# Seven products instead of eight in nine more pairs of a feed-forward, and down-projection sums that begin at 2x in PSUM

## The chip, the core and the metric

The kernel runs on one core of a Trainium2 chip. The metric is device time in microseconds (us) from the start of the program to its end. Times quoted are the median of three runs, or one profiled execution where a trace is read.

The engines go by the profile's names: PE multiplies matrices (PEld is its weight load), DVE and ACT are the vector and the scalar engine, POOL a third elementwise engine, SP issues most transfers.

## The reference

A decoder layer over 256 tokens of width 2048, in float32: a feed-forward, a mixer (sliding-window attention beside RWKV-7), cross-attention, a second feed-forward, a last RMS norm. Both feed-forwards have an inner width of 5632 and compute

```python
def swiglu(h, w_gate, w_up, w_down):
    return (jax.nn.silu(h @ w_gate) * (h @ w_up)) @ w_down

x = x + 0.5 * swiglu(rms_norm(x, ffn1_norm[l]), ffn1_w_gate[l], ffn1_w_up[l], ffn1_w_down[l])
...
x = x + 0.5 * swiglu(rms_norm(x, ffn2_norm[l]), ffn2_w_gate[l], ffn2_w_up[l], ffn2_w_down[l])
```

## The kernel before

**A product.** Every float32 operand is split into a high part (ACT casts it to fp32r, L365, or L373 for the sums below) and a low part (DVE subtracts, L366 or L374). One product of a 128x128 block of activations with a 128x512 block of weights is then three matmuls: high times high (L442), low weight times high (L443), high weight times low activation (L444), added up in one PSUM bank of 128x512 (`times`).

**Pairs of seven.** The 256 tokens are two tiles, t = 0 and 1. `product_pair` works on two weight blocks of 512 columns at once: w_gate and w_up for the same columns (`gate_and_up`), or two column blocks of w_down (`down`). It goes through K in pairs q of two 128-row chunks. A plain pair takes 2 tiles x 2 weight blocks x 2 chunks = 8 products, 24 matmuls. A pair in the set `seven` takes 7 products, 21 matmuls (Strassen's scheme in Winograd's form), named p1 to p7. For that DVE builds four sums of the two weight blocks (L394 to L397, 128x512 each) and these are split again (`two_parts`: two casts on ACT, two subtractions on DVE of 128x1024); in return half of the split of the second weight block falls away (`split_unit(u, slice(1, 2))`). Sums of activations are made once per activation (`combinations`): four per seven pair, and two for each plain pair that comes ahead of the last seven pair.

**Banks.** PSUM has three rings: `mm` (p1, p3, p5; three banks), `acc` (p2, p4, q; three), `tr` (p6, p7, and the transposes of `feat`; two). p5's early plain products go to a bank of their own, `q`, where the activations' sums were not made for these pairs.

**Blocks.** Inner width 5632 is 11 blocks of 512, j = 0 to 10, in three groups of 4, 4 and 3. Block 0 is done plain; blocks 1 to 10 each are one `gate_and_up` of 8 pairs. After a group come two `down` calls (columns 0 to 1023, then 1024 to 2047) over the group's inner columns: 8 pairs, or 6 in the third group. In the second feed-forward the very last call is replaced by plain products. Before, gate and up take seven products in pairs 0, 2, 4 (first feed-forward) or 0, 2, 3, 4 (second, where pair 3's weight sums were computed in the mixer and are loaded); `down` takes them in 2, 4, 6 (groups of 4, first call) and in 2, 4 elsewhere.

**Order.** `next_item` splits the weights of one pair ahead of the pair that PE is on. Other work (transposes of a finished block, sums of activations, norms) is in generators that `bg.tick()` advances between products; `middle`, after the last seven pair of a block, spawns the transposes of the block before (`c["next"]`, L582 and L583). The order of each engine's queue is set when the program is built: instructions are moved there by their estimated readiness, within what the dependencies allow. On the chip each engine runs its queue in order.

**The end of `down`.** With u2 and u3 as helper tiles, ACT copies p1 (L606), and DVE adds p1, p5, p6, p7 and q up and then adds half of each sum to x: twelve DVE instructions of 128x512 a call (L603, L611 to L613).

## Time and profile before

| | us |
|---|---|
| median of 3 runs (2217.76 to 2218.34) | 2218.07 |
| the profiled execution, whole | 2216.97 |
| its span, first to last instruction | 2215.2 |
| PE busy | 2200.2 |
| weight loads busy | 1817.0 |
| DVE busy | 1829.0 |
| ACT busy | 1250.0 |

The first feed-forward takes the span from 5 to 710 us, the mixer and cross-attention 710 to 1508, the second feed-forward 1509 to 2206. "Busy" is a share of the span over stages of different kinds; a matmul's record lasts longer than the time to the next one's start, since they are pipelined, so a rate is read from starts. DVE and ACT records overlap a little in the same way. In a line of the timeline the bracket at the end gives the idle time ahead of an instruction and what ended it.

### The profile page before, as it was taken

Reading aid. Unit: us, or ns where it says so; the run is one execution under the profiler, and the core shown is the slowest. Engines: PE = TensorE matmul, PEld = TensorE weight load, DVE = VectorE, ACT = ScalarE, POOL = GpSimd, SP = SyncE. Lnnn points to the kernel's source line nnn. Section 1 sums busy time; section 2 is a strip of 40 time slices with the busy share of each in tenths; the row PEclk is TensorE's granted clock in tenths of the full one; section 3 lists DMA queues with packets and bytes.
Section 4 is the critical chain, followed back from the end, with each engine's and each line's share of the span. In section 5 each row is a group of like instructions: output and inputs, shape, how many; then the busy total and the mean of one; then the engine's idle time right before and its main releaser. Section 6 shows DMA issues by size and latency. Waiting matters only on the chain.

```text
span 2215.2 us, 28140 instructions
## 1 busy us (share of the span) xinstructions
PE 2200.2 (99%) x10520; PEld 1817.0 (82%) x10520; DVE 1829.0 (83%) x2348; ACT 1250.0 (56%) x1621; POOL 107.0 (5%) x185
## 2 busy tenths in 40 slices
PE   9999999999999999999999999999999999999998
PEld 7888888888888877788888888888888888888886
DVE  7999988898989476977667666558999999999997
ACT  7555555555556477644544546556565565555654
POOL 0000000000000000000331130001000000000000
PEclk9999999999999999999999999999999999999999
DMA  8555555555556545676768687547665666665573
GB/s 306 199 207 198 194 200 201 198 199 194 200 194 204 178 130 165 197 237 210 223 224 287 209 273 270 183 164 280 220 221 190 212 227 211 214 208 208 200 244 135
DMA packets 231560, 466.02 MB, mean 210 GB/s; under 512 B 15520, under 2 KB 17920, under 8 KB 231424
## 3 DMA queue, kind: packets, MB, share of 16 engines
q1 hardware_dynamic: 222256, 438.08, 58.4%
q0 software_dynamic: 7648, 23.52, 3.5%
q10 hardware_dynamic: 1520, 2.63, 0.3%
q8 instruction: 82, 1.34, 0.3%
q14 instruction: 54, 0.44, 0.1%
HBM read 440.49 MB, written 23.59 MB: 209 GB/s over the span
## 4 chain that ended last, share of the span: by engine, by line
PE 94%; DVE 3%; DMA 1%; issue 1%; ACT 1%; SPq 0%; POOLq 0%; POOL 0%; DVEq 0%; ACTq 0%
PE acc L442 19%; PE acc L443 19%; PE acc L444 19%; PE mm L443 8%; PE mm L444 8%; PE mm L442 8%; PE tr L443 2%; PE tr L630 2%; PE tr L442 2%; PE tr L444 2%; PE mm L1425 1%; DVE lo L366 1%; DMA raw<-in_ffn_w_up_dram 1%; PE tr L1355 0%; ACT hi L365 0%
## 5 line engine op out<-in xcount | busy, mean ns | idle before, releaser
L365 ACT CAST hi<-raw 128x1024 fp32r<-128x1024 f32 (+1 forms) x768 | 755.1, 993 | 687.7 <-PE acc L444 485.9
L366 DVE TENSOR_TENSOR lo<-raw,hi 128x1024 fp32r<-128x1024 f32 (+1 forms) x768 | 878.8, 1147 | 291.8 <-ACT hi L365 289.3
L442 PE MATMUL acc<-hi,xhi 128*128 128x512 f32 (+1 forms) x1134 | 445.7, 394 | 2.0 <-DVE ga L1278 1.5
L443 PE MATMUL acc<-lo,xhi 128*128 128x512 f32 (+1 forms) x1134 | 439.9, 388 | 0.8 <-DVE lo L366 0.8
L444 PE MATMUL acc<-hi,xlo 128*128 128x512 f32 (+1 forms) x1134 | 439.7, 388 | 0.0
L442 PEld LDWEIGHTS acc<-hi,xhi 128*128 128x128 f32 x1134 | 213.2, 188 | 47.8 <-issue 3.1
L444 PEld LDWEIGHTS acc<-hi,xlo 128*128 128x128 f32 x1134 | 212.9, 188 | 43.5 <-issue 0.4
L443 PEld LDWEIGHTS acc<-lo,xhi 128*128 128x128 f32 x1134 | 213.4, 188 | 42.7 <-DVE lo L366 2.2
L373 ACT CAST thi<-raw 128x1024 fp32r<-128x1024 f32 x192 | 200.3, 1052 | 69.1 <-DVE raw L396 45.0
L374 DVE TENSOR_TENSOR tlo<-raw,thi 128x1024 fp32r<-128x1024 f32 x192 | 232.1, 1217 | 0.9 <-ACT thi L373 0.3
L442 PE MATMUL mm<-hi,xhi 128*128 128x512 f32 x402 | 156.6, 389 | 0.1
L443 PE MATMUL mm<-lo,xhi 128*128 128x512 f32 x402 | 156.5, 389 | 0.0
L444 PE MATMUL mm<-hi,xlo 128*128 128x512 f32 x402 | 156.4, 389 | 0.0
L444 PE MATMUL acc<-hi,hlo 128*128 128x512 f32 x372 | 145.4, 391 | 0.0
L443 PE MATMUL acc<-lo,hhi 128*128 128x512 f32 x372 | 145.3, 391 | 0.0
L442 PE MATMUL acc<-hi,hhi 128*128 128x512 f32 x372 | 145.0, 390 | 0.0
L442 PEld LDWEIGHTS mm<-hi,xhi 128*128 128x128 f32 x402 | 75.4, 188 | 16.2 <-ACT hi L365 0.5
L443 PEld LDWEIGHTS mm<-lo,xhi 128*128 128x128 f32 x402 | 75.5, 188 | 15.8
L444 PEld LDWEIGHTS mm<-hi,xlo 128*128 128x128 f32 x402 | 75.5, 188 | 15.7
L442 PEld LDWEIGHTS acc<-hi,hhi 128*128 128x128 f32 x372 | 69.9, 188 | 14.3
L443 PEld LDWEIGHTS acc<-lo,hhi 128*128 128x128 f32 x372 | 69.8, 188 | 14.3
L444 PEld LDWEIGHTS acc<-hi,hlo 128*128 128x128 f32 x372 | 69.9, 188 | 14.0
(443 smaller groups left out, 3526.6 us busy)
## 6 DMA issues: line engine op xcount, KB each, us to landing
raw<-in_ffn_w_down_dram SPq DMA_DIRECT2D x88, 1024.0 KB, 5.2
raw<-in_ffn_w_gate_dram SPq DMA_DIRECT2D x84, 1024.0 KB, 5.1
raw<-in_ffn_w_up_dram SPq DMA_DIRECT2D x78, 1024.0 KB, 6.0
raw<-in_w_in_dram SPq DMA_DIRECT2D x136, 512.0 KB, 3.8
raw<-in_w_out_dram SPq DMA_DIRECT2D x32, 512.0 KB, 4.7
raw<-sums SPq DMA_DIRECT2D x20, 512.0 KB, 6.2
raw<-in_w_proj_attn_dram SPq DMA_DIRECT2D x16, 512.0 KB, 4.0
raw<-in_w_proj_rwkv_dram SPq DMA_DIRECT2D x16, 512.0 KB, 5.7
```

What stands on the lines that cost most here:

```text
L365: at["hi"] = act.copy(hi[:, s], raw[:, s])
L366: at["lo"] = dve.tensor_tensor(lo[:, s], raw[:, s], f32(hi[:, s]), ALU.subtract)
L373: act.copy(hi[:], v[:])
L374: dve.tensor_tensor(lo[:], v[:], f32(hi[:]), ALU.subtract)
L442: pe.matmul(o, xh, hi, start=first, stop=False, **how)
L443: pe.matmul(o, xh, lo, start=False, stop=False, **how)
L444: pe.matmul(o, xl, hi, start=False, stop=last, **how)
L630: pe.transpose(b[:, o : o + P], tok[:, t, col : col + P], ident[:])
L1425: pe.matmul(vb[to, (o + k) * P : (o + k + 1) * P][:, r], lhs(k, e), v[:, k, r], start=v is u and k + e == 0, stop=True, **ek,)
```

## The change

Five blocks of gate and up in the first feed-forward (3, 5, 7, 9, 10) take seven products in pair 6 as well. For them the activations' sums of pair 6 are made too, those of pair 5 are not, so pair 5's share of p5 goes to bank q and DVE adds q in at the end. In groups of four the second `down` call takes seven products in pair 6 as well, in both feed-forwards.

`down` no longer adds x at the end for each bank: before its first product, ACT writes 2x into the banks of p2, p4, p3 and q, the products add onto that, and the end takes half of each bank. u2 and u3 are not used there any more; eight DVE instructions a call remain, and ACT has four more. A seven pair now waits for its own sums of activations only, not for all of them. Two 128x128 tiles that nothing reads go.

```diff
@@ -37,6 +37,7 @@
 
 
 SEVEN, SEVEN_DOWN = (0, 2, 4), ((2, 4, 6), (2, 4))
+SEVEN_MORE, MORE = (0, 2, 4, 6), (3, 5, 7, 9, 10)
 SEVEN_2, STAGED = (0, 2, 3, 4), (3,)
 
 STAGE_AT = [266 + 2 * n for n in range(10)]
@@ -89,13 +90,14 @@
                 for w in (wg, wu):
                     yield w, 0, KD, 0, 512
             else:
-                yield (wg, wu), 0, KD, (j * 512, j * 512), SEVEN_2 if last else SEVEN
+                seven = SEVEN_2 if last else SEVEN_MORE if j in MORE else SEVEN
+                yield (wg, wu), 0, KD, (j * 512, j * 512), seven
         yield (wd, wd), 4 * j0, 4 * nj, (0, 512), SEVEN_DOWN[nj < 4]
         if last and (j0, nj) == GROUPS[-1]:
             for n in (2, 3):
                 yield wd, 4 * j0, 4 * nj, n * 512, 512
         else:
-            yield (wd, wd), 4 * j0, 4 * nj, (1024, 1536), SEVEN_DOWN[1]
+            yield (wd, wd), 4 * j0, 4 * nj, (1024, 1536), SEVEN_DOWN[nj < 4]
 
 
 def weight_plan(a):
@@ -194,7 +196,6 @@
-    cpool.tile([P, P], F32, name="shift")
@@ -239,7 +240,6 @@
-    cpool.tile([P, P], F32, name="pad")
@@ -451,21 +451,19 @@
                 k + i == 0, k + i == nk - 1,
             )
 
-    def combinations(sp, x: Act, seven, name, ready=lambda: True, early=True, n=0):
-
-
-
-        pairs = [q for q in range(max(seven) + 1) if early or q in seven]
-        n = n or sum(4 if q in seven else 2 for q in pairs)
+    def combinations(sp, x: Act, seven, name, ready=lambda q: True, less=(), n=0):
+
+
+
+        pairs = sorted((*seven, *less))
+        n = n or 4 * len(seven) + 2 * len(less)
         parts = [sp.tile([P, n, P], F32R, tag=name + e, name=name + e) for e in ("hi", "lo")]
-        c = {"parts": parts, "at": {}, "done": False, "seven": seven, "early": early}
+        c = {"parts": parts, "at": {}, "seven": seven, "less": less}
 
         def work():
             o = 0
-            while not ready():
-                yield
             for q in pairs:
-                while not {2 * q, 2 * q + 1} <= x.done:
+                while not ({2 * q, 2 * q + 1} <= x.done and ready(q)):
                     yield
                 t = wp.tile([P, KU, 512], F32, tag="raw", name="raw", bufs=4)
                 v = t[:, 0].rearrange("p (k t n) -> p k t n", k=2, t=2)
@@ -494,12 +492,10 @@
                 c["at"][q] = o
                 o += n
                 yield
-            c["done"] = True
-
         bg.spawn("mem", work())
         return c
 
-    def product_pair(x: Act, c, w, first, middle, out):
+    def product_pair(x: Act, c, w, first, middle, out, onto=()):
 
 
 
@@ -512,6 +508,11 @@
         b, begun = {}, set()
         rings = {"p1": mm, "p3": mm, "p5": mm, "p2": acc, "p4": acc, "q": acc}
 
+        for to, there in onto:
+            b[to] = rings[to]()
+            act.activation(b[to][:], there, AF.Copy, scale=2.0)
+            begun.add(to)
+
         def add(to, x_, w_, last=False):
             if to not in b:
                 b[to] = rings.get(to, tr)()
@@ -531,7 +532,7 @@
         for q in range(nk // KU):
             k = KU * q
             if q in seven:
-                bg.until(lambda: c["done"] and (q > min(seven) or not bg.groups["feat"][1]))
+                bg.until(lambda: q in c["at"] and (q > min(seven) or not bg.groups["feat"][1]))
                 g, u, s = next_item()
                 end = q == max(seven)
                 ta, tb = s
@@ -552,8 +553,8 @@
             g, u = next_item()
             early, last = q < max(seven), q == nk // KU - 1
             for to, t, wt in (("p2", 0, g), ("p4", 1, g), ("p3", 0, u), ("p5", 1, u)):
-                less = to == "p3" and early and c["early"]
-                if to == "p5" and early and not c["early"]:
+                less = to == "p3" and early and q in c["less"]
+                if to == "p5" and early and q not in c["less"]:
                     to = "q"
                 for i in range(KU):
                     add(
@@ -589,36 +590,36 @@
                 act.activation(hb[:, t], hb[:, t], AF.Silu, scale=r[t])
             else:
                 v = u3 if t else u2
-                dve.tensor_tensor(v[:], b[to][:], v[:], ALU.add)
+                for z in (to, "q") if t and "q" in b else (to,):
+                    dve.tensor_tensor(v[:], b[z][:], v[:], ALU.add)
                 dve.scalar_tensor_tensor(hb[:, t], v[:], r[t], hb[:, t], ALU.mult, ALU.mult)
 
         product_pair(x, c, w, first, middle, out)
         return hb
 
-    def down(sp, h: Act, c, w, xs):
-
-        u2, u3 = sums_of(sp)
-
-        def half(x_, v):
-            dve.scalar_tensor_tensor(x_, v, 0.5, x_, ALU.mult, ALU.add)
+    def down(h: Act, c, w, xs):
+
+        (x00, x01), (x10, x11) = xs
+
+        def half(x_, v, y):
+            dve.scalar_tensor_tensor(x_, v, 0.5, y, ALU.mult, ALU.add)
 
         def first(b):
-            act.copy(u3[:], b["p1"][:])
-            half(xs[0][0], b["p1"][:])
-            half(xs[1][1], b["q"][:])
+            act.activation(x00, b["p1"][:], AF.Copy, scale=0.5)
 
         def middle(b):
-            dve.tensor_tensor(u2[:], b["p6"][:], u3[:], ALU.add)
-            dve.tensor_tensor(u3[:], b["p7"][:], u2[:], ALU.add)
-            dve.tensor_tensor(u2[:], b["p5"][:], u2[:], ALU.add)
-            half(xs[1][0], u3[:])
-            half(xs[1][1], u3[:])
-            half(xs[0][1], u2[:])
+            half(x01, b["p6"][:], x00)
+            half(x10, b["p7"][:], x01)
+            half(x01, b["p5"][:], x01)
+            half(x11, b["q"][:], x10)
 
         def out(b, to):
-            half(xs[int(to in ("p4", "p5"))][int(to in ("p3", "p5"))], b[to][:])
-
-        product_pair(h, c, w, first, middle, out)
+            x_ = xs[int(to in ("p4", "p5"))][int(to in ("p3", "p5"))]
+            half(x_, b[to][:], x_)
+
+        product_pair(
+            h, c, w, first, middle, out, (("p2", x00), ("p4", x10), ("p3", x01), ("q", x11))
+        )
 
     def feat(tok, cols):
 
@@ -727,8 +728,12 @@
                 sp.tile(shape, dt, tag=tag, name=tag, bufs=bufs)
         begun = at["item"]
         c = combinations(
-            sp, norm.x, SEVEN_2 if last else SEVEN, "c",
-            lambda: at["item"] > begun + (4 if last else 7) and not (last and norm.r is None),
+            sp, norm.x, SEVEN_2 if last else SEVEN_MORE, "c",
+            lambda q: (
+                at["item"] > begun + (4 if last else 26 if q > 4 else 7)
+                and not (last and norm.r is None)
+            ),
+            less=(1,) if last else (1, 3),
         )
         c["next"] = []
         for gi, (j0, nj) in enumerate(GROUPS):
@@ -736,7 +741,7 @@
                 [sp.tile([P, 16, T], F32R, tag="hhi", name="hhi")],
                 [sp.tile([P, 16, T], F32R, tag="hlo", name="hlo")], 16,
             )
-            ch = combinations(sp, h, SEVEN_DOWN[nj < 4], "d", early=False, n=12)
+            ch = combinations(sp, h, SEVEN_DOWN[nj < 4], "d", n=12)
 
             def transposed(hb, c):
                 banks = [feat(hb, [2 * q * P, (2 * q + 1) * P]) for q in range(2)]
@@ -787,7 +792,7 @@
                             )
                             done(m, t, cs)
                     continue
-                down(sp, h, ch, wd, [[col(t, n + i) for i in range(2)] for t in range(2)])
+                down(h, ch, wd, [[col(t, n + i) for i in range(2)] for t in range(2)])
                 if end:
                     done(n)
                     done(n + 1)
```

The change moves instructions on DVE and PE; two places are shown, as the engines' queues hold them.

DVE, first feed-forward, before: the end of block 5, from the last sum after its third seven pair. lo is the low part of a weight tile, hlo that of transposed results (tr is the bank they come from), tlo that of a weight sum; L394 to L397 make the weight sums of the next block's first pair.

```order
L581 TENSOR_TENSOR u<-mm,u 128x512
L366 TENSOR_TENSOR lo<-raw_2689,hi 128x1024
L636 TENSOR_TENSOR hlo<-tr,hhi 128x512 x2
L366 TENSOR_TENSOR lo<-raw_2737,hi 128x1024
L394 TENSOR_TENSOR raw<-raw_2820,raw_2772 128x512
L395 TENSOR_TENSOR raw<-raw_2820 128x512
L396 TENSOR_TENSOR raw<-raw_2820,raw 128x512
L366 TENSOR_TENSOR lo<-raw_2689,hi 128x1024
L397 TENSOR_TENSOR raw<-raw_2772,raw 128x512
L374 TENSOR_TENSOR tlo<-raw,thi 128x1024
L366 TENSOR_TENSOR lo<-raw_2737,hi 128x1024
L374 TENSOR_TENSOR tlo<-raw,thi 128x1024
```

After, DVE at the same place, now with a fourth seven pair (pair 6) just behind it; u and hb hold the block's sums and its result.

```order
L582 TENSOR_TENSOR u<-mm,u 128x512
L374 TENSOR_TENSOR tlo<-raw,thi 128x1024
L366 TENSOR_TENSOR lo<-raw_2794,hi 128x1024
L366 TENSOR_TENSOR lo<-raw_2843,hi 128x512
L374 TENSOR_TENSOR tlo<-raw,thi 128x1024
L589 TENSOR_TENSOR hb<-acc,hb 128x512
L637 TENSOR_TENSOR hlo<-tr,hhi 128x512
L589 TENSOR_TENSOR hb<-acc,u 128x512
L637 TENSOR_TENSOR hlo<-tr,hhi 128x512
L594 TENSOR_TENSOR u<-mm,u 128x512 x2
L595 SCALAR_TENSOR_TENSOR hb<-u,rs,hb 128x512
L594 TENSOR_TENSOR u<-acc,u 128x512
```

Before, the two hlo of the block before are read out of tr two pairs ahead of the block's end, in front of the next block's weight sums; after, they stand behind these (both tlo), within the last pair, and a third L594 adds q.

PE, before: the first seven pair of the first `down` call of group 0 (dhi and dlo are the two parts of its sums of activations, hhi and hlo those of the activations themselves).

```order
L442 MATMUL tr<-thi,dhi 128x512 x2
L442 MATMUL mm<-hi,hhi 128x512
L443 MATMUL mm<-lo,hhi 128x512
L444 MATMUL mm<-hi,hlo 128x512
L443 MATMUL tr<-tlo,dhi 128x512
L444 MATMUL tr<-thi,dlo 128x512
L443 MATMUL tr<-tlo,dhi 128x512
L444 MATMUL tr<-thi,dlo 128x512
```

After, PE at the same pair (its p1, p2 and p3 are already under way when the first row is reached):

```order
L442 MATMUL mm<-hi,dhi 128x512
L442 MATMUL acc<-hi,hhi 128x512 x2
L443 MATMUL mm<-lo,dhi 128x512
L444 MATMUL mm<-hi,dlo 128x512
L442 MATMUL mm<-hi,hhi 128x512
L442 MATMUL tr<-thi,dhi 128x512 x2
L442 MATMUL mm<-hi,hhi 128x512
L443 MATMUL tr<-tlo,dhi 128x512
L444 MATMUL tr<-thi,dlo 128x512
L443 MATMUL tr<-tlo,dhi 128x512
L444 MATMUL tr<-thi,dlo 128x512
```

Before, the first matmul with a low weight sum (tlo) is the 54th of the `down` call, five behind the first with a high one (thi); after it is the 64th, since products of this pair that need no weight sum, and the next pair's high parts, are taken ahead.

## The prediction

> **What bounds the kernel now.** The page's first rows, its shares of the span, and the chain that ended last come first.
>
> ```profile
> span 2215.2 us, 28140 instructions
> PE 2200.2 (99%) x10520; PEld 1817.0 (82%) x10520; DVE 1829.0 (83%) x2348; ACT 1250.0 (56%) x1621; POOL 107.0 (5%) x185
> PE 94%; DVE 3%; DMA 1%; issue 1%; ACT 1%; SPq 0%; POOLq 0%; POOL 0%; DVEq 0%; ACTq 0%
> ```
>
> PE is busy 99% of the time and makes up 94% of the chain. Busy alone doesn't say whether a matmul fewer is worth its time, so the rate has to be seen. PE's timeline at the head of group 0's first `down` call shows a stretch without a gap, and then the first seven pair:
>
> ```profile
> 184.63 0.39 PE L444 MATMUL mm<-hi,hlo 128*128 128x512 f32 x1
> ...
> 191.43 0.39 PE L444 MATMUL acc<-hi,hlo 128*128 128x512 f32 x1
> ...
> 192.57 0.39 PE L444 MATMUL mm<-hi,hlo 128*128 128x512 f32 x1
> 192.93 0.50 PE L443 MATMUL tr<-tlo,dhi 128*128 128x512 f32 x1
> 193.27 0.39 PE L444 MATMUL tr<-thi,dlo 128*128 128x512 f32 x1
> ```
>
> Between the first two rows lie 30 steps in 6.80 us: 0.2267 us from one matmul's start to the next. At 192.57 the next start comes after 0.36 us, and the one behind it after 0.34: together 0.25 us more than two plain steps. That is what a low part (tlo) that is late by a moment costs: the only loss in some 40 us.
>
> The same question by stage is asked of the table by windows (PE, PEld, DVE, ACT busy): blocks 5 and 6, group 1's gate and up as a whole, its two `down` calls, and a block of the second feed-forward.
>
> ```profile
> 306.90:349.00 42.10, 42.10 (x191) 34.96 (x190) 38.42 (x47) 23.98 (x28) 0.00 (x0) 1.00 0.58 200
> 349.00:391.20 42.20, 42.20 (x192) 35.02 (x191) 38.01 (x49) 23.17 (x27) 0.00 (x0) 1.00 0.57 199
> 264.70:433.40 168.70, 168.70 (x758) 139.80 (x757) 149.78 (x183) 94.91 (x106) 0.00 (x0) 1.00 0.58 200
> 433.40:475.70 42.30, 42.30 (x191) 34.67 (x190) 40.76 (x54) 23.25 (x26) 0.00 (x0) 1.00 0.58 198
> 475.70:518.20 42.50, 42.50 (x189) 35.21 (x188) 40.14 (x49) 21.87 (x23) 0.00 (x0) 1.00 0.58 199
> 1847.00:1889.00 42.00, 42.00 (x189) 34.33 (x189) 41.07 (x53) 25.48 (x30) 0.00 (x0) 1.00 0.63 219
> ```
>
> A block of gate and up takes 42.2 us (168.7 / 4), in which DVE works 37.4 (149.78 / 4), so 89%; in `down` it works 40.1 to 40.8 of 42.4, 95% and more. ACT has some 18 us free everywhere. So PE sets the pace, at the full clock (the 1.00), and DVE is the one behind it with little room.
>
> **What is removed.** A seven pair has 21 matmuls where a plain one has 24. Five blocks get one more seven pair, and so do four `down` calls (groups 0 and 1 of both feed-forwards): 9 x 3 = 27 matmuls fewer. At 0.2267 us that is 6.1 us, all on the path, as no gap stands around them. The transposes and loads stay as they were (the same weights come in; SP's queue only issues them).
>
> The Trainium skill has another price for the step ("TensorE: Matmul & The Clock Gate", Back-to-back issue gap: about 216 ns for 512 columns, warm). By it the saving would be 5.8 us; the trace's 226.7 ns decides here, and the sum goes by that.
>
> **What is added on DVE and ACT.** DVE's own timeline just ahead of that seven pair carries the prices:
>
> ```profile
> 175.75 1.22 DVE L366 TENSOR_TENSOR lo<-raw,hi 128x1024 fp32r<-128x1024 f32 x1 [1.49 <-ACT hi L365]
> 178.43 1.23 DVE L366 TENSOR_TENSOR lo<-raw,hi 128x1024 fp32r<-128x1024 f32 x1 [0.26 <-ACT hi L365]
> 179.57 1.28 DVE L592 TENSOR_TENSOR u<-mm,u 128x512 f32<-128x512 f32 x2
> ...
> 187.71 0.28 DVE L481 TENSOR_TENSOR raw<-raw 128x128 f32<-128x128 f32 x1
> 187.91 0.68 DVE L395 TENSOR_TENSOR raw<-raw 128x512 f32<-128x512 f32 x1
> ...
> 190.46 0.68 DVE L493 TENSOR_TENSOR dlo<-raw,dhi 128x512 fp32r<-128x512 f32 x1
> 191.06 0.68 DVE L397 TENSOR_TENSOR raw<-raw,raw 128x512 f32<-128x512 f32 x1
> 191.66 1.22 DVE L374 TENSOR_TENSOR tlo<-raw,thi 128x1024 fp32r<-128x1024 f32 x1
> 192.79 0.68 DVE L366 TENSOR_TENSOR lo<-raw,hi 128x512 fp32r<-128x512 f32 x1
> 193.40 1.22 DVE L374 TENSOR_TENSOR tlo<-raw,thi 128x1024 fp32r<-128x1024 f32 x1
> ```
>
> From start to start an instruction of 128x512 takes 0.60 us (190.46, 191.06, 191.66), one of 128x1024 1.13 (191.66, 192.79), one of 128x128 0.20. One more seven pair costs DVE four sums and two low parts, less half a low part: 4 x 0.60 + 2 x 1.13 - 0.53 = 4.1 us. In the five blocks comes the addition of q, 0.6. So such a block asks DVE for 37.4 + 4.7 = 42.1 us, while PE's part of it falls to 42.2 - 0.7 = 41.5. DVE is 0.6 us short in each. Blocks 4, 6 and 8 between them leave it 4.8 us (42.2 - 37.4); only 9 and 10 follow each other. On the total alone, the split of a pair ahead takes 0.6 us up. So the total costs nothing; what costs is the order.
>
> `down` gives DVE four instructions a call back, 2.4 us, and where a call gets a third seven pair it pays 4.1: 40.1 + 1.7 = 41.8 of PE's 41.8 on the busiest reading of the second call, but with no loss seen at 95%. PE waited for none of the instructions taken out, so their going brings nothing by itself.
>
> ACT gets four writes of 2x into PSUM a call. No row shows such a write; the nearest are the copy out of PSUM and the scaled copy in SBUF:
>
> ```profile
> L606 ACT COPY u<-mm 128x512 f32<-128x512 f32 x11 | 6.5, 587 | 10.4 <-PE mm L444 10.4
> L1744 ACT ACTIVATE x<-x,rs x4: 706/714/724, 2205.1 to 2209.7; 128x512 f32<-128x512 f32 x4
> ```
>
> So 4 x 0.59 to 0.71, 2.3 to 2.8 us in a call in which ACT has some 19 free. The write has to wait for its bank, and the casts of the next weights stand behind it. The banks of p2 and p4 come free with the first two half-additions of the call before, 2 x 6 products' matmuls ahead of its end; the new p2 is needed 18 matmuls, 4.1 us, after its old bank was full, and DVE's addition and ACT's write need 0.6 + 0.7. It costs nothing unless DVE stands some 2.5 us behind there.
>
> **Where the order costs.** Two places, both shown in the queues above.
>
> First, the first `down` of each group of the first feed-forward, behind blocks 3, 7 and 10, each of which now has its fourth seven pair. There the low parts of the block before (two, 1.2 us), the sums of activations made from them (0.6 + 4 x 0.2 + 0.6 = 2.0) and q (0.6) have moved behind the last seven pair: 3.8 us of DVE work more ahead of the first tlo that `down` needs. Against it stand the 1.75 us that DVE idles there now (1.49 + 0.26 in the brackets), and ten matmuls that PE takes ahead, 2.3 us. On balance nothing is lost. If the idle time can't be used, 3.8 - 2.3 = 1.5 us are lost in each. I take 0.5, nearer the low end, since the idle time is in the trace: 3 x 0.5 = 1.5 us.
>
> Second, PE's queue holds many more seven pairs in which products are taken out of their written order around a late low part: 42, where there were 15. Six of the 27 belong to the first place. Each of the others costs between nothing (the reordering hides it all) and the 0.25 us of the row at 192.57. Being ordered around the lateness is what makes most of them free; I take a quarter of the price: 21 x 0.06 = 1.3, and for the two starts of blocks 4 and 8 in the second feed-forward, which is at 98% of DVE already (41.07 of 42.0), 0.1 each, 1.5 in all. The bounds are 0 and 21 x 0.25 = 5.3.
>
> **The sum.** -6.1 + 1.5 + 1.5 = -3.1 us. The profiled execution, 2216.97 us whole with 2215.2 of span and 1.8 around it, would be 2213.9. The median stands 1.1 above that execution, so 2218.07 - 3.1 = 2215.0. With every bound at its best it is 2218.07 - 6.1 = 2212.0, at its worst 2218.07 - 6.1 + 4.5 + 5.3 = 2221.8. About 0.2%, 4.4 us, is what a measurement of this kernel can tell from no change: 2213.6 and 2222.5.
>
> **The rivals.**
>
> *Nothing is lost.* The order hides all that DVE is late, as it does in the 40 us around 192.57 but for 0.25. For it: group 1 shows a DVE at 95% in `down` without loss. Against: the five blocks ask for over 100%. 2212.0.
>
> *Each late low part costs its price.* Then 27 x 0.25 = 6.6 us come back and it is 2218.07 - 6.1 + 6.6 = 2218.6: no change. For it: the one place of the row paid in full although PE's order already went around it. Against: there are 15 such places now, and PE is still without gaps over whole blocks.
>
> *DVE sets the pace: slower.* Its place is the end of the five blocks. The transposed results leave the two tr banks only behind the next block's weight sums, and p6 and p7 of that block, or of `down`, need these banks. If DVE comes there late by what the block has more than before, 4.7 us, and its idle time elsewhere can't be used since it is bound to ACT's casts, and these to PE's releases, then each of the five blocks pays 4.7: 23.5 - 6.1, 2235.5. It decides from the point at which 10.5 of the 23.5 us are paid, 2.1 a block. The rows that tie them:
>
> ```profile
> DVE lo L366 <- ACT hi L365: 289.3, 258, 3.5
> ACT hi L365 <- PE acc L444: 485.9, 356, 3.9
> ```
>
> For it: these are DVE's longest waits, 289 us, and behind them ACT's for PE. Against: in a block DVE comes to its first tlo some us ahead, and 0.6 us short is not 2.1.
>
> The Trainium skill would lean this way ("Perfetto Trace Analysis", Identifying the Most-Contended Engine: TensorE is to be judged by the busy share of its weight loads, the others by occupancy, and the highest is worked on first). By it DVE's 83% stands above PE's 82%, and work put on DVE would show. The starts 0.2267 us apart without gaps speak against it on the whole, the 100% in five blocks for it there.
>
> That the change doesn't do what it says is no case: the queue of PE holds 27 matmuls fewer.
>
> **How the numbers follow.** The forecast, some of the saving given back: 0.46, its own range 2213.0 to 2217.2. Nothing lost: 0.32. Each paid in full: 0.10. DVE's pace: 0.12. The likeliest is 2215.0. The range reaches over the first three, from 2211.8 to 2220.5, and leaves out DVE's pace and little else. Faster by over 0.2%: nearly all of "nothing lost" and the low end of the forecast, 0.31 + 0.06 = 0.37. Slower: 0.12. Within: 0.51.
>
> **What would show it.** In the profile after, the matmuls still 0.227 apart, 27 fewer; block 5 at 41.5 to 42 us with DVE above 41; the first seven pair of each first `down` with a gap of up to some 0.8 us ahead of its L443; L513 with its 44 writes off the chain. The forecast is wrong if PE's gaps in the two feed-forwards grow by less than 1.5 us or more than 5, or if the rest of the program moves at all: nothing between the two feed-forwards changes place.

## The result and the profile after

The changed kernel takes 2225.91 us (median of 7 runs, 2224.03 to 2226.27), the kernel before 2218.22 (7 runs, 2217.76 to 2219.14). The ratio is 1.0032, interval 1.0022 to 1.0042: 7.7 us slower, where 3.1 us faster had been forecast. With the 6.1 us of the matmuls that are gone, 13.8 us were lost, not 3.0.

The page of the profiled execution (2226.11 us) opens with the span, the busy time of each engine and the chain that ended last:

```profile
span 2224.4 us, 28208 instructions
PE 2199.9 (99%) x10493; PEld 1809.7 (81%) x10493; DVE 1841.4 (83%) x2369; ACT 1283.6 (58%) x1684; POOL 107.2 (5%) x185
PE 84%; DVE 8%; DMA 4%; ACT 2%; issue 1%; SPq 0%; POOLq 0%; POOL 0%; DVEq 0%; ACTq 0%
```

PE's records are 27 fewer, as the queue says. Its busy share, 99%, says nothing of the loss; the chain does: PE falls from 94% to 84%, DVE rises from 3% to 8% and DMA from 1% to 4%.

The table by windows (PE, PEld, DVE, ACT busy) for group 1: its gate and up, and its first and second `down` call:

```profile
267.66:436.80 169.14, 168.09 (x750) 138.13 (x749) 159.44 (x194) 97.98 (x112) 0.00 (x0) 1.00 0.60 202
437.03:481.80 44.77, 43.29 (x191) 34.64 (x190) 42.53 (x59) 26.63 (x33) 0.00 (x0) 1.00 0.53 180
481.80:523.58 41.78, 41.78 (x185) 34.36 (x184) 35.84 (x44) 23.33 (x25) 0.00 (x0) 1.00 0.59 194
```

Gate and up takes 169.1 us where it took 168.7 with six matmuls more, DVE works 159.4 of them, 94%, where it was 149.8. The first `down` has grown from 42.3 to 44.8 us.

Where the time goes is read best from PE's own timeline. Here it is at the first `down` of group 0, whose first matmul starts at 181.07 (before, at 179.86):

```profile
194.28 0.39 PE L442 MATMUL mm<-hi,dhi 128*128 128x512 f32 x1
194.51 0.39 PE L442 MATMUL acc<-hi,hhi 128*128 128x512 f32 x1
195.58 0.50 PE L442 MATMUL acc<-hi,hhi 128*128 128x512 f32 x1 [0.68 <-ACT hi L365]
196.47 0.50 PE L443 MATMUL mm<-lo,dhi 128*128 128x512 f32 x1 [0.39 <-DVE lo L366]
...
197.26 0.61 PE L442 MATMUL tr<-thi,dhi 128*128 128x512 f32 x2
198.33 0.50 PE L442 MATMUL mm<-hi,hhi 128*128 128x512 f32 x1 [0.46 <-ACT hi L365]
198.81 0.50 PE L443 MATMUL tr<-tlo,dhi 128*128 128x512 f32 x1
```

Starts that should lie 0.23 us apart lie 1.07 and 0.89 apart, 0.85 ahead of the row at 198.33 (from the second matmul of the row at 197.26) and 0.48 behind it. In PE's queue products that were expected to be ready first stand ahead of their written order; then there are no more of them, and PE waits for hi, lo, hi and tlo in turn. The first `down` of groups 1 and 2 has the same four steps (1.07, 0.86, 0.83 and 0.47 us in both, to 0.02). DVE's timeline shows why (line, operation, in brackets the idle time before it):

```profile
187.61 0.74 DVE L595 SCALAR_TENSOR_TENSOR hb<-u,rs,hb 128x512 f32<-128x512 f32 x1
190.17 1.23 DVE L366 TENSOR_TENSOR lo<-raw,hi 128x1024 fp32r<-128x1024 f32 x1 [1.81 <-ACT hi L365]
191.32 1.28 DVE L637 TENSOR_TENSOR hlo<-tr,hhi 128x512 fp32r<-128x512 f32 x2
192.51 0.68 DVE L472 TENSOR_TENSOR raw<-hhi,hlo 128x512 f32<-128x512 f32 x1
193.11 0.69 DVE L394 TENSOR_TENSOR raw<-raw,raw 128x512 f32<-128x512 f32 x1
...
197.54 1.22 DVE L374 TENSOR_TENSOR tlo<-raw,thi 128x1024 fp32r<-128x1024 f32 x1
```

The last instruction of the block (L595) starts 6.5 us after the `down` call's first matmul. Before, the second of two such stood there:

```profile
180.77 1.41 DVE L593 SCALAR_TENSOR_TENSOR hb<-u,rs,hb 128x512 f32<-128x512 f32 x2
179.86 0.39 PE L442 MATMUL acc<-hi,hhi 128*128 128x512 f32 x1
```

That one started at about 181.4, 1.6 us after 179.86. So DVE comes 5 us later to the block's end. Behind that it idles 1.81 us ahead of 190.17, since the low part at the head of its queue waits for a cast, and ACT's cast for PE to free its buffer:

```profile
189.09 1.05 ACT L365 CAST hi<-raw 128x1024 fp32r<-128x1024 f32 x1 [1.90 <-PE acc L444]
```

Behind it stand the low parts of the block that has just ended and the sums of activations for pair 6 (L637, L472), and only then the weights' sums (L394) that the first tlo needs. That tlo starts 16.5 us after the call's first matmul (197.54 less 181.07); before, it was 11.8 (191.66 less 179.86). It is 4.7 us later, and PE has 2.3 us of other matmuls to put in: 2.4 us are lost.

The second place is the start of a group, 2 to 3 us in. PE, and DVE around it:

```profile
270.18 0.39 PE L444 MATMUL acc<-hi,xlo 128*128 128x512 f32 x1
271.27 0.47 PE L442 MATMUL acc<-thi,xhi 128*128 128x512 f32 x1 [0.70 <-DVE x L605]
```

```profile
259.35 0.69 DVE L394 TENSOR_TENSOR raw<-raw,raw 128x512 f32<-128x512 f32 x1 [2.35 <-DMA raw<-in_ffn_w_up_dram]
...
270.44 1.28 DVE L605 SCALAR_TENSOR_TENSOR x<-acc,x 128x512 f32<-128x512 f32 x2
```

PE waits for an accumulator that the additions of the second `down`'s last pair (L605) release. DVE had idled 2.35 us for the weights of the next block's pair 0; when they landed, eight additions of `down` (L605) and the sums and low parts of pair 0 came due together. At the start of block 6, behind block 5 with its fourth seven pair, it is the same with the additions of the block (0.5 us lost; at block 10 it is 0.3):

```profile
342.00 0.69 DVE L394 TENSOR_TENSOR raw<-raw,raw 128x512 f32<-128x512 f32 x1 [1.77 <-DMA raw<-in_ffn_w_up_dram]
353.23 0.50 PE L442 MATMUL acc<-hi,xhi 128*128 128x512 f32 x1 [0.34 <-DVE hb L589]
```

The profiled execution also came to its first seven pair 1.3 us later than that of before. PE's rows there, of before, after, `seeds` and `seeds_third` (the first two experiments below):

```profile
52.08 0.73 PE L442 MATMUL tr<-thi,chi 128*128 128x512 f32 x2 [0.26 <-ACT thi L373]
53.42 0.73 PE L442 MATMUL tr<-thi,chi 128*128 128x512 f32 x2 [0.26 <-ACT thi L373]
53.21 0.74 PE L442 MATMUL tr<-thi,chi 128*128 128x512 f32 x2 [0.26 <-ACT thi L373]
52.05 0.73 PE L442 MATMUL tr<-thi,chi 128*128 128x512 f32 x2 [0.26 <-ACT thi L373]
```

The last two kernels have the same code up to there and differ by 1.2 us, so this is a matter of the run and no part of the 13.8.

For the whole, each stage's length on PE's timeline less 0.2267 us for each of its matmuls gives an excess: what the stage loses, and the transposes of finished blocks on top, about 0.11 us each from start to start. They make 0.9 us of a `down` of groups 0 and 1 (8 transposes), 2.6 of gate/up 1 (24), 1.7 of gate/up 2 (16) and 3.5 of down 2 (32; before 2.6, as 24), so the kernel before loses next to nothing from the first `down` on in the first feed-forward, and a difference between two rows is what counts. This is the excess in us in one profiled execution of each kernel, for those below too (`down` stands for a group's two calls; the 0.8 us of the eight more transposes in the third group's `down` come back at the head of the mixer):

| kernel | down 0 | gate/up 1 | down 1 | gate/up 2 | down 2 | second ffn, gate/up 1 |
|---|---|---|---|---|---|---|
| before | 1.2 | 2.7 | 1.2 | 1.8 | 3.1 | 3.5 |
| after | 3.6 | 4.8 | 3.8 | 3.7 | 6.2 | 4.6 |
| seeds | 1.2 | 2.7 | 1.2 | 1.8 | 4.4 | 3.5 |
| seeds_third | 1.2 | 3.5 | 1.2 | 2.1 | 4.0 | 4.5 |
| more59 | 1.7 | 4.5 | 1.2 | 3.3 | 4.3 | 5.0 |
| more_two | 3.6 | 3.5 | 3.6 | 2.3 | 6.3 | 3.7 |
| late_sums | 1.4 | 4.2 | 1.4 | 3.7 | 4.4 | 4.9 |
| third_245 | 0.9 | 2.8 | 0.9 | 1.8 | 4.0 | 3.7 |
| after_245 | 2.5 | 3.4 | 2.4 | 2.7 | 6.3 | 4.0 |
| more3710_245 | 2.5 | 2.8 | 2.4 | 1.8 | 6.3 | 4.3 |
| blocks_0245 | 1.3 | 4.1 | 1.5 | 3.5 | 4.3 | 4.6 |
| late_245 | 2.9 | 3.4 | 2.9 | 2.6 | 4.5 | 4.1 |
| all_0245 | 1.4 | 4.0 | 1.4 | 3.2 | 4.7 | 4.7 |
| three_0245 | 1.5 | 2.8 | 1.5 | 1.8 | 4.4 | 4.0 |

From before to after the first `down` calls lose 2.4 and 2.6 us and the third, against `seeds`, 1.8: 6.9 us together, half of all. Gate/up 1 and 2 lose 2.0 and 1.9 more, at the group starts and at blocks 6 and 10, and gate/up 1 of the second feed-forward 1.0: there it isn't the group's start but the start of block 7 and two pairs behind it (steps of 0.72 at 1902 us and 0.41 at 1918 us).

### The profile page after: what moved, and what is told of

The parts are those of the page before. It is cut to its first block, busy times and chain, and to the rows that moved or that the text cites. A ratio compares the mean times of both kernels' runs of the same rounds, so it can differ in the third digit from the quotient of the medians.

```text
span 2224.4 us, 28208 instructions
## 1 busy us (share of the span) xinstructions
PE 2199.9 (99%) x10493; PEld 1809.7 (81%) x10493; DVE 1841.4 (83%) x2369; ACT 1283.6 (58%) x1684; POOL 107.2 (5%) x185
## 4 chain that ended last, share of the span: by engine, by line
PE 84%; DVE 8%; DMA 4%; ACT 2%; issue 1%; SPq 0%; POOLq 0%; POOL 0%; DVEq 0%; ACTq 0%
PE acc L442 17%; PE acc L443 17%; PE acc L444 17%; PE mm L443 7%; PE mm L444 7%; PE mm L442 7%; DVE lo L366 3%; PE tr L443 2%; PE tr L444 2%; PE tr L631 2%; PE tr L442 2%; DMA raw<-in_ffn_w_up_dram 2%; DMA raw<-in_ffn_w_down_dram 2%; PE mm L1430 1%; ACT hi L365 1%
## 5 line engine op out<-in xcount | busy, mean ns | idle before, releaser
L373 ACT CAST thi<-raw 128x1024 fp32r<-128x1024 f32 x210 | 219.1, 1051 | 70.0 <-DVE raw L396 42.4
L374 DVE TENSOR_TENSOR tlo<-raw,thi 128x1024 fp32r<-128x1024 f32 x210 | 254.5, 1218 | 1.4 <-ACT thi L373 0.9
L443 PE MATMUL mm<-lo,xhi 128*128 128x512 f32 x377 | 146.9, 390 | 0.0
L442 PE MATMUL mm<-hi,xhi 128*128 128x512 f32 x377 | 146.8, 390 | 0.0
L444 PE MATMUL mm<-hi,xlo 128*128 128x512 f32 x377 | 146.8, 389 | 0.0
L394 DVE TENSOR_TENSOR raw<-raw,raw 128x512 f32<-128x512 f32 x95 | 65.2, 686 | 29.8 <-DMA raw<-in_ffn_w_up_dram 15.2
L442 PEld LDWEIGHTS mm<-hi,xhi 128*128 128x128 f32 x377 | 70.8, 188 | 15.2 <-ACT hi L365 0.5
L443 PEld LDWEIGHTS mm<-lo,xhi 128*128 128x128 f32 x377 | 70.8, 188 | 14.7
L444 PEld LDWEIGHTS mm<-hi,xlo 128*128 128x128 f32 x377 | 70.8, 188 | 14.7
```

Of the source, the lines that this page charges most:

```text
L373: act.copy(hi[:], v[:])
L374: dve.tensor_tensor(lo[:], v[:], f32(hi[:]), ALU.subtract)
L394: dve.tensor_tensor(t[1][:, 0], ru[:, 0], rg[:, 0], ALU.subtract)
L442: pe.matmul(o, xh, hi, start=first, stop=False, **how)
L443: pe.matmul(o, xh, lo, start=False, stop=False, **how)
L444: pe.matmul(o, xl, hi, start=False, stop=last, **how)
```

## The experiments

Each was measured in five rounds beside the kernel before, whose median was 2217.8 to 2218.4 in them. A ratio of theirs is uncertain by about 0.0009 either way, 2 us, and so is a difference of two medians below.

**The parts of the change, one by one.** Without any fourth seven pair and with two in each second `down`:

```
-SEVEN_MORE, MORE = (0, 2, 4, 6), (3, 5, 7, 9, 10)
+SEVEN_MORE, MORE = (0, 2, 4), ()
-            yield (wd, wd), 4 * j0, 4 * nj, (1024, 1536), SEVEN_DOWN[nj < 4]
+            yield (wd, wd), 4 * j0, 4 * nj, (1024, 1536), SEVEN_DOWN[1]
```

> The new writes of 2x into PSUM and the shorter additions of `down` alone: no fourth seven pair in any block, no third one in a second `down`; all 10520 matmuls of before. Theory (what was lost lies in the order that the extra seven pairs make): no change, 2218.2 +- 1, the gaps of PE in the first feed-forward as before (each first `down` 0.5 to 0.7 us, each later group start none). Rival (the writes hold ACT's casts and the banks up): 3 to 5 us slower, 2221 to 2223, with PE's gaps at the head of the `down` calls.

2218.06 us, ratio 1.0001 (0.9992 to 1.0010). Without a fourth seven pair the writes of 2x cost nothing that this can tell, as forecast. How long one takes, in the changed kernel (minimum, median, maximum in ns):

```profile
L513 ACT ACTIVATE acc<-x x33: 577/586/603, 180.2 to 2150.7; 128x512 f32<-128x512 f32 x33
L513 ACT ACTIVATE mm<-x x11: 589/602/604, 172.8 to 2131.4; 128x512 f32<-128x512 f32 x11
```

Next, only the first of the two edits (no fourth seven pair, but the third one in the second `down`):

> As the kernel with the writes alone, and a third seven pair in the four second `down` calls: 12 matmuls, 2.7 us fewer. Theory (the third seven pair takes raw buffers, so that the loads of the next block come late and PE waits some 1.0 us for an accumulator at the start of three of the four groups that follow): 2218.2 - 2.7 + 3.0 = 2218.5, with the gap of some 1 us about 2.5 us after the start of each such group. Rival (that gap in the changed kernel comes from the blocks' fourth pairs): no gap there, 2215.5.

2216.68 us, 0.9995 (0.9987 to 1.0004), between the two. Of the 2.7 us of twelve matmuls 1.4 were had. The excess grows by 0.8 and 0.3 in gate/up 1 and 2, at the group starts, though no block has a fourth pair here: the theory's place. Of the 1.0 in gate/up 1 of the second feed-forward 0.3 lie at the group's start and the rest at the start of block 7, 130 us in. Gate/up 2 of the second feed-forward gained 1.3, which neither had.

The fourth pair in blocks 5 and 9 alone:

```
-SEVEN_MORE, MORE = (0, 2, 4, 6), (3, 5, 7, 9, 10)
+SEVEN_MORE, MORE = (0, 2, 4, 6), (5, 9)
```

> The changed kernel with the fourth seven pair in blocks 5 and 9 alone, and not in the last block of a group (3, 7, 10): 9 matmuls, 2.0 us more than the changed kernel. Theory (the last block of a group leaves DVE 4.9 us behind, and of that 2.4 us a time are lost in the first `down`, 7.1 in all): 2225.9 + 2.0 - 7.1 = 2220.8, each first `down` back at a loss of 0.5 to 0.7 us. Rival (the five blocks ask DVE for more than there is, and each costs alike, so that the time is lost wherever DVE comes last): the ten us over the three group starts and the program's start are shared by five blocks, 2.0 each: 2225.9 + 2.0 - 3 x 2.0 = 2221.9, with losses inside blocks 5 and 9 of some 2 us each.

2218.55 us, 1.0002 (0.9993 to 1.0011), below both. Taking the pair out of blocks 3, 7 and 10 gives 7.4 us back and puts nine matmuls in: 9.4 us lost for three pairs, 6.5 of it, by the table, in the `down` stages; groups 0 and 1 are back at 1.2 to 1.7. Blocks 5 and 9 seem to cost too: 1.9 us over `seeds_third` with 1.4 us of matmuls less, though that is no more than the uncertainty; the excess of gate/up 1 and 2 grows by 1.0 and 1.2.

The changed kernel with two seven pairs in the second `down` (the second edit alone):

> The changed kernel with two seven pairs in the second `down` calls, as before: 12 matmuls, 2.7 us more than the changed kernel. Theory (the third one costs 1.0 us at three group starts): 2225.9 + 2.7 - 3.0 = 2225.6, no change, and no gap at the group starts. Rival (the gap there is not of its making): 2228.6 with the gaps still there.

2223.89 us, 1.0027 (1.0017 to 1.0038), below both. Twelve matmuls more, and 2.0 us faster: beside blocks with a fourth pair the third one in `down` costs more, 4.7 us, than alone. The gaps at the group starts are gone, as the theory has it, and so is that at block 7 of the second feed-forward (4.8 to 3.5, 3.7 to 2.3, 4.6 to 3.7: 3.6 of the 4.7).

**Order or total?** The changed kernel's instructions, with the sums of pair 6's activations behind the weights' sums of the first seven pair:

```
+gone = set()
...
                 g, u, s = next_item()
+                gone.add(x)
...
-            ch = combinations(sp, h, SEVEN_DOWN[nj < 4], "d", n=12)
+            ch = combinations(
+                sp, h, SEVEN_DOWN[nj < 4], "d",
+                lambda q, m=max(SEVEN_DOWN[nj < 4]), h=h: q < m or h in gone, n=12,
+            )
```

> The changed kernel, with the sums of activations of the last seven pair of a `down` (and with them the low parts of the block before) put behind the weights' sums of its first seven pair in DVE's queue: same instructions, another order. Theory (in the first `down` DVE comes 4.9 us later to the first tlo than before, 2.3 us more than PE can take ahead; 2.0 us of that are these sums, 1.2 the low parts): 3 x 2.3 us come back, 2225.9 - 6.9 = 2219.0, at most 2221, and the gaps 13 us after the start of each first `down` are gone. Rival (DVE is short by its total in and after such a block, whatever stands first): the gap moves to a later pair, 2225.9 within 1.

2219.02 us, 1.0002 (0.9993 to 1.0010): the 6.9 us came back. That they did so to the tenth is chance, at an uncertainty of 2 us; by the table the `down` stages give 6.6 back. DVE in the same `down` (lines are two or three higher in this kernel: L396 to L399 are the weights' sums, L376 the low part tlo, L640 hlo, L474 the activations' sum):

```profile
187.15 0.75 DVE L598 SCALAR_TENSOR_TENSOR hb<-u,rs,hb 128x512 f32<-128x512 f32 x1
187.82 0.69 DVE L396 TENSOR_TENSOR raw<-raw,raw 128x512 f32<-128x512 f32 x1
...
190.86 1.28 DVE L640 TENSOR_TENSOR hlo<-tr,hhi 128x512 fp32r<-128x512 f32 x2
...
192.65 1.22 DVE L376 TENSOR_TENSOR tlo<-raw,thi 128x1024 fp32r<-128x1024 f32 x1
...
198.20 0.69 DVE L474 TENSOR_TENSOR raw<-hhi,hlo 128x512 f32<-128x512 f32 x1
```

The block ends as late as in the changed kernel (187.15), but the weights' sums use the 1.8 us that were idle, and tlo starts at 192.65 in place of 197.54, 12.0 us after the call's first matmul (180.61) in place of 16.5. The number of instructions on each engine is the same, so a DVE short by its total could not have given this back.

The first seven pair of `down` put one pair later:

```
-SEVEN, SEVEN_DOWN = (0, 2, 4), ((2, 4, 6), (2, 4))
+SEVEN, SEVEN_DOWN = (0, 2, 4), ((3, 4, 6), (2, 4))
```

> The changed kernel with the `down` calls' seven pairs at 3, 4 and 6 in the place of 2, 4 and 6 (groups 0 and 1): the first one has one plain pair, 24 matmuls or 5.4 us, more ahead of it. Theory (the late DVE of a group's last block is a backlog that one plain pair lets it work off, some 3 us a pair): the gaps at the first seven pair go in groups 0 and 1, 2 x 2.3 us back, 2225.9 - 4.6 = 2221.3; pairs 3 and 4 follow each other, and such a pair asks DVE for 6.4 us while PE has 4.8, 1.6 short, which its lead has to cover, else up to 1.6 in each of eight calls. Rival (the backlog isn't worked off, DVE being short in `down` as well): the gap stands at pair 3, 2225.9 or more.

2225.05 us, 1.0031 (1.0020 to 1.0043): of the 4.6 us that the theory had, nothing that this can tell. At pair 3 the loss is nearly gone, as the theory says (one step of 0.34 us at the first tlo), but at pair 4 right behind PE stands 1.1 us, and near the end of the second `down` two steps of 0.9 and 1.1 us are new. One plain pair nearly works the backlog off; two seven pairs in a row bring it back.

**The group starts.** Five buffers in place of four in the ring `raw`, no fourth seven pair:

```
-            t = [wp.tile([P, KU, 512], F32, tag="raw", name="raw", bufs=4) for _ in range(2)]
+            t = [wp.tile([P, KU, 512], F32, tag="raw", name="raw", bufs=5) for _ in range(2)]
...
-            less=(1,) if last else (1, 3),
+            less=() if last else (1, 3),
```

> The kernel with the writes and the third seven pair in the second `down` calls, no fourth one in the blocks, with five raw buffers in the place of four. To make room, the second feed-forward's blocks take no sums of activations for pair 1 (q in their place), and two small rings have two buffers, so the first feed-forward is what is compared. Theory (the weights' sums of the seven pair at a block's or group's start wait 1.8 to 2.4 us for a load whose buffer came free late, and then stand ahead of the additions that release PE's accumulators): the 0.76 and 0.26 us lost at the starts of groups 1 and 2 of the first feed-forward go, 2216.7 - 1.0 = 2215.7. Rival (DVE is short there in any case): they stay, 2216.7.

2228.68 us, 1.0046 (1.0034 to 1.0059): 12 us slower than with four, which neither theory had. The excess is not in gaps: the matmuls themselves lie farther apart (below), because what was saved for room had moved the stage's tiles by 64 bytes. So the run said nothing of the buffers, and was made again with the tiles of the feed-forwards where they had been, and those of the mixer where they were:

```
-    def aligned(sp):
+    def aligned(sp, n=32):
 
-        return sp.tile([P, 16], F32, name="shift")
+        return sp.tile([P, n], F32, name="shift")
...
-        aligned(sp)
+        aligned(sp, 16)
```

> The kernel with five raw buffers, which came out 12 us slower than with four, with the tiles of the two feed-forwards 64 bytes higher in each partition, where they were with four (the two small rings had taken 64 bytes from what lies below them). Theory (the matmuls of `down` in that kernel, 229.3 ns apart on the mean in place of 226.7, were slow by the place of hi against hhi, thi and dhi): 226.7 ns again, and then the gaps at the group starts gone: 2215.7 plus up to 1.5 for the q additions of the second feed-forward, 2216 to 2217. Rival (the fifth buffer slows them, by more loads or writes at a time): 2228.7.

2221.49 us, 1.0017 (1.0008 to 1.0026). The matmuls' pace is back, 226.9 ns in the first feed-forward against 228.9 (the mean over starts under 0.2385 us apart). The run is still 4.8 us slower than `seeds_third`, 4 of them between the two feed-forwards (972.1 us against 968.0), where it wasn't meant to be compared. The gaps at the group starts are still there, 0.9 and 0.8 us, and DVE idles 2.58 us for the load. The ring theory falls: the fifth buffer serves the sums, while the feed-forwards' loads have a ring of their own (`raw2`). The load is a little late all the same: SP issues it 15.6 us ahead of group 1 in `seeds` and 14.7 ahead in `seeds_third`, and it lands 10.5 and 8.7 us ahead. A fifth buffer for the loads wasn't tried.

The `down` calls' pairs at 2, 4 and 5, no fourth seven pair:

```
-SEVEN, SEVEN_DOWN = (0, 2, 4), ((2, 4, 6), (2, 4))
+SEVEN, SEVEN_DOWN = (0, 2, 4), ((2, 4, 5), (2, 4))
```

> The kernel with the writes and the third seven pair, no fourth one in the blocks, with the `down` calls' seven pairs at 2, 4 and 5 in the place of 2, 4 and 6 in groups 0 and 1: two plain pairs, not one, lie between the last seven pair of a second `down` and pair 0 of the next block. Theory (a seven pair at 6 and one at 0 are too near to each other for DVE, with a block's end between): the losses at the group starts (0.76, 0.26, 0.97) go, 2216.7 - 2.0 = 2214.7. Rival (two in a row, at 4 and 5, are worse: 6.4 us of DVE work in 4.8 us each): up to 1.6 us in each of eight calls, 2216.7 + 12.8 - 2.0 = 2227.5 at the worst.

2214.87 us, 0.9983 (0.9974 to 0.9992): as the theory had it, to well within the uncertainty, and faster than both kernels. DVE has the additions of `down` to do while the load is on its way, and doesn't idle ahead of the weights' sums:

```profile
254.97 0.68 DVE L605 SCALAR_TENSOR_TENSOR x<-acc,x 128x512 f32<-128x512 f32 x1
255.57 1.22 DVE L366 TENSOR_TENSOR lo<-raw,hi 128x1024 fp32r<-128x1024 f32 x1
256.70 0.69 DVE L394 TENSOR_TENSOR raw<-raw,raw 128x512 f32<-128x512 f32 x1
```

The weights' sums start 8.0 us ahead of the group here (256.70, the group at 264.67), later than the 8.6 of `seeds_third` (255.37, the group at 264.00), and nothing is lost: what decides is not the load by itself but that four additions of `down` no longer stand behind it. The two seven pairs in a row cost nothing here: the `down` stages stand at 0.9, which is their transposes.

**Can the fourth seven pair pay?** The same edit on the whole changed kernel:

> The changed kernel, all five blocks and the third seven pairs as they are, with the `down` calls' seven pairs at 2, 4 and 5 in groups 0 and 1. The sums of activations that stood ahead of the first seven pair (those of pair 6) are no longer made there, and two plain pairs lie ahead of the next block's pair 0. Theory (order, not total): the 2.3 us in the first `down` of groups 0 and 1 and the gaps of 0.9 us at three group starts go; group 2, with its own pairs 2 and 4, keeps its 2.3. 2225.9 - 4.6 - 2.7 = 2218.6. Rival (DVE's total in the five blocks): the loss turns up elsewhere, 2225.9.

2219.46 us, 1.0008 (0.9999 to 1.0017), 6.5 us faster than the changed kernel with the same number of instructions on each engine. The group starts' gaps go, the first `down` calls keep 1.6 of their 2.3 us: the sums for pairs 4 and 5 both come from block 2 and stand ahead of the block's last additions and of the first tlo. The largest step, 0.82 us, is a wait for a write of 2x, which waits for the addition of q in its bank:

```profile
186.25 0.50 PE L442 MATMUL acc<-hi,hhi 128*128 128x512 f32 x1 [0.43 <-ACT acc L513]
185.59 0.60 ACT L513 ACTIVATE acc<-x 128x512 f32<-128x512 f32 x1 [0.70 <-DVE u L594]
```

So behind a block with a fourth pair the writes can come onto the path.

Without blocks 5 and 9:

```
-SEVEN_MORE, MORE = (0, 2, 4, 6), (3, 5, 7, 9, 10)
+SEVEN_MORE, MORE = (0, 2, 4, 6), (3, 7, 10)
```

> The kernel with the writes, the third seven pair in the second `down` calls and pairs 2, 4 and 5 there, with a fourth seven pair in blocks 3, 7 and 10 alone: 9 matmuls, 2.0 us fewer than the 2214.9 measured without it. Theory (a block ahead of a `down` whose first seven pair has nothing else of DVE ahead of it loses 0.2 to 0.4 us): 2214.9 - 2.0 + 2 x 0.3 + 2.3 in group 2, whose pairs are as before = 2215.8. Rival (a fourth pair in a block costs its 1 us and more anywhere, as at blocks 5 and 9): 2214.9 - 2.0 + 2 x 1.1 + 2.3 = 2217.4.

2218.57 us, 1.0003 (0.9994 to 1.0011), 2.8 us above the theory and 1.2 above the rival. The excess in gate/up 1 and 2 is that of no fourth pair (2.8, 1.8): in blocks 7 and 10 the fourth pair costs nothing in the block, and a group's last block with one costs 1.5 to 2.3 us in the `down` behind it, where the theory had 0.3 in two of three.

The late sums and the pairs 2, 4, 5 together:

> The changed kernel with both other orders in the `down` calls: seven pairs at 2, 4 and 5 in groups 0 and 1, and the sums of activations of a call's last seven pair behind the weights' sums of its first. Theory (the two losses are separate): the 2219.0 of the late sums less the 0.5, 0.7 and 0.9 us at the group starts, 2216.9. Rival (the 1.6 us that the first `down` still lost with pairs 2, 4 and 5 comes from the order of pairs, not from the sums): 2219 to 2220.

2221.01 us, 1.0012 (1.0003 to 1.0021), 4 us above the theory, above the rival too, and slower than either order by itself. The gap at the first seven pair goes; the loss moves to the second of two in a row:

```profile
208.27 0.40 PE L444 MATMUL mm<-hi,dhi 128*128 128x512 f32 x1
209.71 0.73 PE L444 MATMUL tr<-thi,dhi 128*128 128x512 f32 x2 [1.03 <-ACT thi L375]
```

The sums that were put late now stand in the queue just ahead of two pairs that follow each other, and DVE has no lead left for them.

The pairs moved in the five blocks alone:

```
-SEVEN_MORE, MORE = (0, 2, 4, 6), (3, 5, 7, 9, 10)
+SEVEN_MORE, MORE = (0, 2, 4, 5), (3, 5, 7, 9, 10)
```

> The changed kernel with pairs 0, 2, 4 and 5 in place of 0, 2, 4 and 6 in the five blocks; same number of instructions of each kind, but for the place of the plain pairs. Theory (a seven pair at 6 stands too near to the block's end and to pair 0 of what follows): the block before is transposed a pair earlier, so DVE comes to the first `down` with less behind it, and two plain pairs lie ahead of pair 0: of the 2.3 us at each first `down` some 1.8 go, and the 0.5 us at the starts of blocks 6 and 10: 2225.9 - 5.4 - 1.0 = 2219.5. Rival (DVE's total in the five blocks, or two seven pairs in a row): 2225.9, or up to 1.6 us more in each of five blocks.

2218.73 us, 1.0002 (0.9993 to 1.0011): 7.2 us faster than the changed kernel with the same number of matmuls and sums. The first `down` calls are back at 1.3 to 1.5, the gaps at blocks 6 and 10 are gone, those at the group starts stay. One thing else changed, against the expectation's "same number of instructions of each kind": with pair 5 a seven pair no plain pair needs bank q any more, and the five additions of q (L594 `u<-acc,u`, 0.6 us each at the block's end) are gone from DVE. How much of the 7.2 us is theirs was not tried.

Both orders moved, with the late sums and then without:

> As the kernel with both other orders in `down`, and with the blocks' four seven pairs at 0, 2, 4 and 5: all 27 matmuls fewer, and all three orders changed. Theory (what was lost lies in the order, not in DVE's total): of the 6.1 us of the matmuls nearly all is had, 2218.1 - 6.1 + 1 to 2 = 2213 to 2214. Rival (DVE short by its total in the five blocks, some 1 us each): 2217.

> As that one, with the fourth seven pair in blocks 3, 7 and 10 alone: 6 matmuls, 1.4 us more. Theory (order): 1.4 us slower than with all five, 2214.5 to 2215.5. Rival (blocks 5 and 9 can't pay in any order, since another block follows that asks as much of DVE): 1 to 2 us faster than with all five.

2219.90 us, 1.0007 (0.9998 to 1.0016), and 2219.79, 1.0007 (0.9999 to 1.0016). Both theories of the first miss, in part by the gap of `late_245`, which the late sums bring along (0.9 us in each group's `down` at pairs 4 and 5). Between the two, blocks 5 and 9 save six matmuls and bring nothing; the second's theory and rival miss alike.

> The changed kernel with pairs 0, 2, 4, 5 in the five blocks and 2, 4, 5 in the `down` calls of groups 0 and 1; the sums of activations stay where they were (putting them late made the sums for pair 5 come too late). All 27 matmuls fewer. Theory (order): the 2218.7 of the blocks' order alone, less the group starts (0.9, 1.0 and 0.9 us): 2215.9. Rival (the sums for pairs 4 and 5, both made behind block 2, stand ahead of the first tlo, as where the `down` calls alone were moved, 1.6 us a first `down`): 2219 to 2220.

2215.59 us, 0.9990 (0.9981 to 0.9999). All 27 matmuls fewer, 10.3 us faster than the change as it was made, by other places for the seven pairs and the five additions of q that go with them. The number is the theory's, but the stages don't bear its sum out: the gaps at the group starts are gone, and new steps stand where pairs 4 and 5 follow each other in a block (0.94 us in place of 0.23 at 417 us), so gate/up 1 stands at 4.0, where `blocks_0245` has 4.1. The profiled execution was the slowest of its runs, 2217.70 us.

> The same with the fourth seven pair in blocks 3, 7 and 10 alone, 6 matmuls or 1.4 us more. Theory (blocks 5 and 9 cost about what they save, as with the late sums, where 2219.9 and 2219.8 were measured): the same as with all five within 0.5. Rival (each seven pair pays in the right order): 1.4 us slower than with all five.

2215.36 us, 0.9989 (0.9980 to 0.9997): the same without blocks 5 and 9. And `third_245`, with no fourth pair and 15 matmuls more than all, is at 2214.87 no slower. The fourth pair saves 0.68 us and, to the 2 us for all five that can be told, costs as much or more in every order that was tried.

## Why the prediction was wrong

**What held.** PE sets the pace, 27 matmuls fewer are 6.1 us; the pace is 227 ns, as taken. An extra seven pair costs DVE 4.7 us in a block by the sum; group 1 shows (159.44 - 149.78) / 2 = 4.8. The writes of 2x take 0.59 to 0.60 us, at the low end of 0.59 to 0.71, and lie off the path in `seeds`; the case that was excepted, a DVE far behind at that place, came in `after_245`. Of the two places named for the order the first, the first `down` calls, is where half of the time went.

**The step that failed** is the first of the two under "Where the order costs": 0.5 us for each first `down`, at most 1.5, where 2.3 us were lost (6.9 in three). It went wrong twice. The work that moves ahead of the first tlo was counted as 3.8 us; on DVE's rows, from 6 us ahead of the call's first matmul to the first tlo, it is 5.0: a sum of the block's own fourth pair (L582, 0.6 us) and the half low part of `down`'s first seven pair (0.5, at 195.73) came to stand there too. And the idle 1.75 us were set against it. They didn't go away: DVE idles 2.1 us in that stretch before and 1.8 after, now at a place where the head of its queue waited for a cast and the cast for PE, with work that could have been done waiting behind it. 5.0 less 0.3 of idle time is the 4.7 us by which the tlo is later, and less the 2.3 that PE can take ahead it is the 2.4 that were lost in group 0. `late_sums` shows that it was the order: with pair 6's sums (2.0 us) behind the weights' sums in place of ahead of them, the loss was gone.

**Two steps had no price at all.** "With no loss seen at 95%", said of the third seven pair in the second `down`, looked at that call's share of DVE (40.14 of 42.50 us is 94%), not at what follows: pair 6 and the next block's pair 0 are two pairs apart, with a block's end between. By the medians it cost 1.3 us of 2.7 alone (`seeds_third` against `seeds`) and 4.7 beside the fourth pairs (`more_two` against after). PE waits there for an accumulator that a late addition frees, and no term of the forecast had that wait. The same meeting at the starts of blocks 6 and 10 was in the forecast only as a displaced pair at 0.06 us; it cost 0.5 and 0.3 us.

**The rivals.** "Each late low part pays" was right that lateness is paid, but it took 0.25 us for each of 27; in fact a few places paid 1 to 2.5 us and most nothing. "DVE sets the pace" had the side and the five blocks' end right, not the mechanism: 13.8 us over five blocks would be 2.8 each, past its point of 2.1, but DVE was busy 94% of group 1's gate and up and wasn't the bound (with the same instructions in another order 6.9 us came back), and PE waited for hi, lo, tlo and accumulators, not for the tr banks. The Trainium skill's "Perfetto Trace Analysis" (Identifying the Most-Contended Engine), which leaned that way, ranks 83% against 82% before and 83% against 81% after; these shares don't show what was lost.

What was left out altogether is the sum over places. Each was judged by whether DVE is over its share; none by how long DVE's queue is at the moment in which PE has no other product to take.

## What to carry to other kernels

An in-order engine with 10% of its time free has no 10% to give: what counts is how much stands in its queue ahead of the one result that the bound engine needs next, and idle time behind a wait at the head of that queue can't be spent. Before adding work, follow the queue over the next two block ends, count all that stands ahead, and spread the added items where the distance is largest; here moving five pairs by one place, which also made five additions needless, was worth 7 us; the fourth pairs themselves brought nothing, and the third ones in `down`, at the right place, some 3 us (`third_245` against `seeds`). Idle time that the trace shows is a credit only if the instruction that would fill it is next in the queue.

## What the runs showed that was not expected

In these runs a matmul's pace hangs on where the tiles lie in SBUF. The kernel with four raw buffers and a third seven pair, with every stage's tiles 64 bytes higher in each partition and not an instruction changed:

> The kernel with the writes and the third seven pair, four raw buffers, with one thing changed: the tiles of all three stages lie 64 bytes higher in each partition; same instructions in the same order. Theory (the pace of a matmul hangs on where its two operands lie): starts in the `down` calls 229 ns apart, some 1 us a call and 8 to 12 us in all, 2225 to 2229. Rival (place does nothing): 2216.7.

2237.97 us, 1.0090 (1.0076 to 1.0104): 21 us slower than without the shift, about twice what the theory had. The groups of PE instructions by line (count, busy us, mean ns), shifted first and unshifted second:

```profile
L443 PE MATMUL acc<-lo,hhi 128*128 128x512 f32 x368 | 145.8, 396 | 0.0
L444 PE MATMUL acc<-hi,hlo 128*128 128x512 f32 x368 | 145.7, 396 | 0.0
```

```profile
L444 PE MATMUL acc<-hi,hlo 128*128 128x512 f32 x368 | 143.8, 391 | 0.0
L443 PE MATMUL acc<-lo,hhi 128*128 128x512 f32 x368 | 143.8, 391 | 0.0
```

Each takes 5 ns more, and the starts in the first feed-forward lie 230.2 ns apart on the mean in place of 227.0. The clock is the same (0.999). The changed kernel is not touched by this: it took away two tiles of 512 bytes, and its matmuls start 227.2 ns apart there, against 226.9 before; the 0.3 may be short waits. Why the place matters wasn't tried. An experiment that changes a buffer's size should look at the pace of the matmuls before it reads anything else from the time.
